# Layer-1 adaLN blocks on VectorE by multiply-and-sum along transposed weights, and layer-norm and square sums moved from GpSimd to VectorE

## The chip, the cores and the metric

One NeuronCore of a Trainium2 chip runs the whole kernel. The metric is the device time of one execution in microseconds; runs of the kernel before and of the changed one are compared by their medians.

## What is computed

Two transformer-like layers run over 384 tokens (128 context tokens, 256 sample tokens) of width 2048. Each layer has an adaLN modulation, one wide input projection that feeds two branches, and one output projection. All of it is fp32. The parts that the change touches:

```
def adaln(cond, w_mod, b_mod):
    m = jax.nn.silu(cond) @ w_mod + b_mod          # (1, 2048) @ (2048, 6144)
    shift, scale, gate = jnp.split(m, 3, axis=-1)
...
for layer in range(2):
    sh, sc, gt = adaln(cond_ctx, w_mod, b_mod)     # context tokens
    hp = rms_norm(xp, g) * (1.0 + sc) + sh
    sh2, sc2, gt2 = adaln(c, w_mod, b_mod)         # sample tokens
    ...
# layer 0, conv branch
a = ga * sigmoid(gb)
a = depthwise_conv(a, conv_w) + conv_b             # 31 taps, 1024 channels
a = silu(layer_norm(a, ln_g, ln_b)) * silu(gate_a)
# layer 0, attention branch: qk-RMSNorm, rotary, dense attention, times silu(gate_b)
# both: concat([a, b]) @ w_out, times gate, added to x
```

So each layer needs 12 vector blocks of adaLN (shift, scale and gate, four blocks of 512 outputs each), and each block is a product of two vectors of 2048 (context and sample condition) with a 2048 x 512 weight block of 4 MB.

## The kernel before, in words

Features lie on partitions (128 at a time, 16 blocks `k`), tokens on the free axis. Every projection (`proj_feat`, 256 output features) streams its weights from HBM in four pieces of 512 KB (`load_w`, pool `raw`, NRAW buffers, SP's queue). ScalarE rounds a piece to its high half `whi`, VectorE subtracts to get the low half `wlo` (both in `split`; three buffers each), and TensorE makes 24 matmuls of 128x384 per piece in `feat_unit` (L354: hi by hi, hi by lo, lo by hi). A piece is called a split below. Projections of layer 0 come in this order: four pairs gate `gb` and value `ga` of the conv branch, then four of gate A, four of gate B, then the eight of the output projection `out_proj`. Results lie in PSUM pairs `pf` (five banks).

Beside the projections, layer 0 has three chains. Attention (`qkv_tile`, `attend`) is emitted behind the second `ga`. The 31-tap convolution (`conv_steps`, L659 on VectorE) starts with each `ga`. When all eight channel blocks are convolved, layer norm follows: `ln_mean` sums the eight blocks into `lsum` and multiplies by ones on TensorE (`mean`), `ln_center` subtracts the mean (L711) and adds squares into `lvar`, `rstd_cols`/`rstd_rows` turn that into `rsl` (TensorE), a power on GpSimd, and `rbl` (TensorE), `ln_out` scales (L721), and L741 multiplies the branch into `mix`. Only then can `out_proj` split `mix` into `hhi`/`hlo` and begin. The buffers `wk` (four) are shared by the squares of the layer norm and by the SiLU results of gate B, in program order.

adaLN blocks are made in two ways. On TensorE: `gemv_block` loads 4 MB through the `raw` pool (SP's queue) and makes 16 matmuls (L139) and four transposes (L172); `pump` issues its pieces at a rate (`R0`, `RA`, `RB`) per unit of weights. On VectorE: `mod_vector` loads eight pieces of 512 KB through GpSimd's queue (`side_load`) into a ring of two slots and runs, for each of 16 `k` and both conditions, one instruction of 128x512 that multiplies by a per-partition scalar and adds to a running sum (L195 the first, L197 the rest). Its `done` transposes the sums on TensorE (`gvt`, L205, eight transposes) and reduces them on VectorE (L207). Layer 1's four shift blocks, the last scale block and four gate blocks are made that way, nine in all; their sums and slots lie in rooms that are free at the time (`mix`, `kT`, `v`, `att`, `apad`).

The order of the instructions on each engine is set by a list scheduler when the program is built: what is ready goes, by priority; the convolution taps and VectorE's adaLN work have a later priority (`later(LATER)`). On the chip each engine takes its own list strictly in order.

Of the kernel before, what the change touches and what calls it, by code (L numbers as in the profile page):

```python
# [19 lines left out]
P = 128  # L20
# [18 lines left out]
NRAW = 7  # L39
# [4 lines left out]
SHIFT_AT = (7, 9, 11)  # L44
RA = 1.35
# [6 lines left out]
def trunk(ctx: ExitStack, tc: tile.TileContext, d: dict, o: dict):  # L52
# [129 lines left out]
    def mod_vector(layer, part, j, av, ring):  # L182
        if (layer, part) not in mods:
            mod_tile(layer, part)
        w = d[f"mod_w{layer}"][4 * part + j]
        av = av.rearrange("p (g f) -> p g f", g=2)
        with later(LATER):
            for u in range(8):
                raw = ring[u % len(ring)].rearrange("p (k f) -> p k f", k=2)
                side_load(raw, w[:, 2 * u:2 * u + 2, :])  # L190
                for i in range(2):
                    k = 2 * u + i
                    for g in range(2):
                        if k == 0:
                            nc.vector.tensor_scalar(av[:, g], raw[:, i], cst[:, 2 * k + g:2 * k + g + 1], None, ALU.mult)  # L195
                        else:
                            nc.vector.scalar_tensor_tensor(av[:, g], raw[:, i], cst[:, 2 * k + g:2 * k + g + 1], av[:, g],  # L197
                                                           ALU.mult, ALU.add)

        def done():  # L200
            sl = slice(4 * j, 4 * j + 4)
            for g in range(2):
                pc = ps_gv.tile([P, 512], F32, tag="gv", name="gvt")
                for i in range(4):
                    ins = nc.tensor.transpose(pc[:, i * P:(i + 1) * P], av[:, g, i * P:(i + 1) * P], ident).ins  # L205
                    tc.add_manual_dep(ins, order["product"].name, NOSYNC, reason="not before its place")
                nc.vector.tensor_reduce(mods[layer, part][:, sl, g:g + 1], pc.rearrange("p (k c) -> p k c", k=4),  # L207
                                        AX.X, ALU.add)
            mod_finish(layer, part, sl, None)
        return done  # L210

# [31 lines left out]
    xT = big.tile([P, KC, T], F32, tag="bigA", name="xT")  # L243

    def square_sum():
        av = tmp.tile([P, T], F32, tag="sacc", name="sacc", bufs=1)

        def each(f):
            if f == 0:
                nc.scalar.activation(av, xT[:, f, :], AF.Square)  # L250
# [480 lines left out]
    for fb in range(4):  # L731
        def ev_a(j, ps, fb=fb):
            if fb == 0 and j == 0:
                shifts.pop(0)()
# [239 lines left out]
```

## Time and profile before

| | |
|---|---|
| three timed runs | 1295.45, 1299.06, 1300.13 us; median 1299.06 |
| profiled execution | span 1295.9 us from its first instruction to its last; the page gives no other time of it |
| busy | PE 98%, DVE 68%, ACT 42%, POOL 11% of the span |
| chain that ended last | PE 85%, DMA 5%, DVE 5%, issue 3% |
| DMA | 252.8 MB, 195 GB/s mean |

A row of a group reads: line, engine, operation, written tile `<-` read tiles, shape, count; then the time in which at least one of them ran (us), the mean of one (ns); then the engine's idle time just before them and what ended it. Busy time of TensorE counts overlapping matmuls as one, so 98% is no measure of its pace: two neighbouring 128x384 matmuls that each last 342 ns start 175 ns apart when nothing holds them.

### The profile page before, as it was taken

The page shows a single profiled execution, that of the slowest core. Times are in us where ns is not written, and L with a number is a line of the kernel's source. Part 1 is how long each engine was busy: PE and PEld are TensorE (multiplying, and loading weights), DVE is VectorE, ACT ScalarE, POOL GpSimd, SP SyncE. Part 2 cuts the span into 40 slices and gives each one's busy share as a digit, 9 for nine tenths or more (in the row PEclk, how much of TensorE's full clock was granted, in tenths as well). Part 3 has the DMA queues.
Part 4 walks back from the last instruction along what each step waited for, and adds up shares of the span by engine and source line. Part 5 has one row for each costly group of instructions (what it writes and reads, how often), then busy time and mean ns, then how long its engine had stood idle before and what let it go on. Part 6 is the DMA issues. An engine that isn't in the chain of part 4 may idle for free.

```text
span 1295.9 us, 18150 instructions
## 1 busy us (share of the span) xinstructions
PE 1267.4 (98%) x7000; PEld 1123.1 (87%) x7000; DVE 882.0 (68%) x1464; ACT 544.5 (42%) x941; POOL 142.2 (11%) x162
## 2 busy tenths in 40 slices
PE   6999999999999999999999999999999999999997
PEld 4566687888887888999999988899999999999997
DVE  2245627899999979989976932454544689996443
ACT  3344433644556645432363633344444422343332
POOL 0210100210000042122220000000000011111110
PEclk9999999999999999999999999999999999999998
DMA  9988867688654566676644444433333577764412
GB/s 364 403 309 313 300 185 258 232 307 295 226 166 160 196 221 218 209 225 217 199 135 130 121 128 130 123 118 109 98 99 103 185 231 229 252 194 146 123 50 98
DMA packets 71222, 252.76 MB, mean 195 GB/s; under 512 B 7456, under 2 KB 11808, under 8 KB 67552
## 3 DMA queue, kind: packets, MB, share of 16 engines
q1 hardware_dynamic: 59920, 211.90, 48.9%
q0 software_dynamic: 11072, 39.60, 9.8%
q8 instruction: 55, 0.90, 0.3%
q14 instruction: 31, 0.25, 0.1%
q10 hardware_dynamic: 144, 0.10, 0.0%
HBM read 247.91 MB, written 3.67 MB: 194 GB/s over the span
## 4 chain that ended last, share of the span: by engine, by line
PE 85%; DMA 5%; DVE 5%; issue 3%; POOL 1%; ACT 1%; SPq 0%; DVEq 0%; POOLq 0%; ACTq 0%
PE pf L354 57%; PE pt L333 10%; PE q L571 6%; PE gv L139 5%; DMA area<-in_mod_w 3%; DVE area L197 2%; PE s_ps L470 2%; PE o_ps L495 2%; DVE wlo L262 1%; DMA raw<-in_wf 1%; PE pT_ps L491 1%; DMA ring<-in_mod_w 1%; PE gv L172 1%; POOL lvar L718 1%; PE y_ps L862 1%
## 5 line engine op out<-in xcount | busy, mean ns | idle before, releaser
L354 PE MATMUL pf<-hhi,whi 128*128 128x384 f32 (+1 forms) x1664 | 569.2, 342 | 0.7 <-ACT whi L261 0.7
L354 PE MATMUL pf<-hlo,whi 128*128 128x384 f32 (+1 forms) x1664 | 569.7, 342 | 0.0
L354 PE MATMUL pf<-hhi,wlo 128*128 128x384 f32 (+1 forms) x1664 | 567.2, 343 | 1.7 <-DVE wlo L262 1.7
L262 DVE TENSOR_TENSOR wlo<-raw,whi 128x1024 fp32r<-128x1024 f32 x256 | 314.8, 1230 | 294.3 <-ACT whi L261 288.9
L261 ACT CAST whi<-raw 128x1024 fp32r<-128x1024 f32 x256 | 268.3, 1049 | 466.3 <-PE pf L354 242.5
L354 PEld LDWEIGHTS pf<-hhi,whi 128*128 128x128 f32 x1664 | 313.1, 188 | 24.0 <-issue 14.2
L354 PEld LDWEIGHTS pf<-hhi,wlo 128*128 128x128 f32 x1664 | 313.3, 188 | 9.8 <-issue 3.2
L354 PEld LDWEIGHTS pf<-hlo,whi 128*128 128x128 f32 x1664 | 313.6, 188 | 5.3 <-issue 2.9
L197 DVE SCALAR_TENSOR_TENSOR area<-area,cst 128x512 f32<-128x512 f32 x240 | 177.8, 777 | 14.7 <-DMA area<-in_mod_w 14.5
L659 DVE SCALAR_TENSOR_TENSOR cv<-apad,cw,cv 128x399 f32<-128x399 f32 x240 | 140.6, 635 | 1.1 <-ACT cv L657 0.8
L91 POOL DMA_DIRECT2D area<-in_mod_w x64 | 34.7, 542 | 424.0 <-DVE area L197 222.0
L333 PE MATMUL pt<-wlo,hhi 128*128 128x512 f32 x192 | 75.8, 395 | 0.0
L254 POOL TENSOR_TENSOR sacc<-sacc,sqf 128x384 f32<-128x384 f32 x43 | 55.2, 1284 | 186.9 <-ACT sqf L253 185.1
L333 PE MATMUL pt<-whi,hhi 128*128 128x512 f32 x192 | 75.7, 397 | 0.0
L333 PE MATMUL pt<-whi,hlo 128*128 128x512 f32 x192 | 75.0, 396 | 0.0
L333 PEld LDWEIGHTS pt<-whi,hhi 128*128 128x128 f32 x192 | 36.0, 188 | 12.4 <-ACT hhi L280 2.5
L571 PE MATMUL q<-whi,hhi 128*128 128x512 f32 x96 | 41.1, 428 | 4.4 <-ACT hhi L267 4.4
L478 ACT ACTIVATE pr<-s_ps,nm 128x384 f32<-128x384 f32 (+1 forms) x48 | 24.4, 509 | 49.7 <-DVE nm L477 34.7
L333 PEld LDWEIGHTS pt<-whi,hlo 128*128 128x128 f32 x192 | 36.0, 188 | 10.1 <-issue 0.8
L333 PEld LDWEIGHTS pt<-wlo,hhi 128*128 128x128 f32 x192 | 36.1, 188 | 9.0 <-issue 0.8
L139 PE MATMUL gv<-ring,cst 128*32 128x512 f32 (+1 forms) x288 | 35.8, 582 | 8.2 <-DMA ring<-in_mod_w 7.6
L571 PE MATMUL q<-wlo,hhi 128*128 128x512 f32 x96 | 40.5, 422 | 0.0
(171 smaller groups left out, 991.8 us busy)
## 6 DMA issues: line engine op xcount, KB each, us to landing
raw<-in_wf SPq DMA_DIRECT2D x144, 512.0 KB, 4.5
ring<-in_mod_w SPq DMA_DIRECT2D x32, 1024.0 KB, 7.5
area<-in_mod_w POOLq DMA_DIRECT2D x64, 512.0 KB, 4.6
raw<-in_w_out SPq DMA_DIRECT2D x64, 512.0 KB, 4.4
raw<-in_mod_w SPq DMA_DIRECT2D x56, 512.0 KB, 5.6
raw<-in_wq SPq DMA_DIRECT2D x32, 512.0 KB, 8.8
raw<-in_wt SPq DMA_DIRECT2D x24, 512.0 KB, 3.6
raw<-in_wkv SPq DMA_DIRECT2D x8, 512.0 KB, 7.8
```

The lines of the kernel that those rows point to most:

```text
L91: ins = nc.gpsimd.dma_start(dst, src).ins
L139: nc.tensor.matmul(ps[32 * g:32 * g + 32, :nf], lhsT=stat(k), rhs=raw[:, i % raw.shape[1], :], start=(k < 4), stop=(k >= KC - 4))
L197: nc.vector.scalar_tensor_tensor(av[:, g], raw[:, i], cst[:, 2 * k + g:2 * k + g + 1], av[:, g], ALU.mult, ALU.add)
L254: nc.gpsimd.tensor_tensor(av, av, s, ALU.add)
L261: nc.scalar.copy(dst_hi, src)
L262: order["split"] = nc.vector.tensor_tensor(dst_lo, src, dst_hi.bitcast(F32), ALU.subtract).ins
L333: nc.tensor.matmul(pp[t], lhsT=x[:, k, tt], rhs=y[:, i, :], start=(k == 0 and n == 0), stop=(k == KC - 1 and n == 2))
L354: ins = nc.tensor.matmul(pp[j][:, :n], lhsT=x[:, i, fj], rhs=y[:, k, :n], start=(begin and k % 8 == 0 and m == 0), stop=(end and k % 8 == ...
L470: nc.tensor.matmul(ps, lhsT=mix[:, h0 + h, t * P:(t + 1) * P], rhs=kT[:, kv, c0:c0 + nk * P], start=True, stop=True)
L495: nc.tensor.matmul(po, lhsT=v[:, slots[j], kv * HD:(kv + 1) * HD], rhs=pT[:, j, :], start=(j == 0), stop=(j == nk - 1))
L571: nc.tensor.matmul(pq[b][t], lhsT=x[:, k, tt], rhs=y[:, 0, 512 * b:512 * b + 512], start=(k == 0 and n == 0), stop=(k == KC - 1 and n == 2))
L659: nc.vector.scalar_tensor_tensor(st["o"], apad[:, c, j:j + CVW], cw[:, c, j:j + 1], st["o"], ALU.mult, ALU.add)
```

## The change

Eight things change together.

- `mod_vector` gives way to `mod_rows`: the modulation weights are also laid out transposed (`modT`, one output per partition), and the two silu'd conditions are kept in every partition (`crow`, 128 x 2 x 2048, two broadcast loads through GpSimd's queue and two SiLU on ScalarE). One `tensor_tensor_reduce` multiplies a 128 x n weight tile with a condition and sums along the free axis into one column of `sm`. n is 2048 (eight per block) or 1024 (sixteen per block, the halves added by L158).
- The four shift blocks use `lent`, the room of `x` (24 KB per partition: two load slots and one for the unread products), right after layer 0 has read `x` for the last time before its residual. `x` is loaded again (`xT2`, 3.1 MB) when they are done. They were the first block in `mix` and three in the rooms of layer norm's time.
- The scale's third block moves from TensorE to VectorE too, so two blocks (scale 2 and 3) use four rooms of 1024 (`kv`, which now holds `kT` and `v` as one, and two `att`). The gate's four blocks use `apad` and `kv`.
- No transposes `gvt` and no reductions L207 remain.
- `lsum`, `lvar` and layer 0's sum of squares `sacc` are added up by VectorE, not GpSimd.
- `NRAW` 7 becomes 6, `RA` 1.35 becomes 1.2, the places of the `done` calls change (`SCALE_AT`).
- Tile `x["T"]` stands for `xT`, since there are two.
- The scratch for GpSimd's DMA descriptors is set to 2048.

```
-NRAW = 7
+NRAW = 6
-SHIFT_AT = (7, 9, 11)
-RA = 1.35
+SCALE_AT = (11,)
+RA = 1.2
...
+    crow = const.tile([P, 2, D], F32, name="crow")
+    def load_crow():
+        for g, name in enumerate(("c_ctx", "c")):
+            side_load(crow[:, g, :], d[f"row_{name}"].rearrange("(a f) -> a f", a=1).broadcast_to([P, D]))
+        for g in range(2):
+            nc.scalar.activation(crow[:, g, :], crow[:, g, :], AF.Silu)
...
+    def mod_rows(layer, part, j, slots):
+        *slots, junk = slots
+        n = junk.shape[1]
+        sm = const.tile([P, 4, 2, D // n], F32, name=f"sm{layer}{part}{j}")
+        with later(LATER):
+            for i in range(4):
+                for h in range(D // n):
+                    raw = slots[turn["n"] % len(slots)]
+                    turn["n"] += 1
+                    side_load(raw, d[f"modT{layer}"][16 * part + 4 * j + i, :, h * n:(h + 1) * n])
                     for g in range(2):
-                        if k == 0:
-                            nc.vector.tensor_scalar(av[:, g], raw[:, i], cst[:, 2 * k + g:2 * k + g + 1], None, ALU.mult)
-                        else:
-                            nc.vector.scalar_tensor_tensor(av[:, g], raw[:, i], cst[:, 2 * k + g:2 * k + g + 1], av[:, g],
-                                                           ALU.mult, ALU.add)
+                        nc.vector.tensor_tensor_reduce(out=raw if g else junk, in0=raw, in1=crow[:, g, h * n:(h + 1) * n],
+                                                       scale=1.0, scalar=0.0, op0=ALU.mult, op1=ALU.add,
+                                                       accum_out=sm[:, i, g, h:h + 1])
...
-    gemv_q.extend(bias_q + mod_part(0, 2) + mod_part(1, 1, (512,) * 3))
+    gemv_q.extend(bias_q + mod_part(0, 2) + mod_part(1, 1, (512,) * 2))
+    lent = big.tile([P, KC * T], F32, tag="bigA", name="lent")
+    slots = [lent[:, i * D:(i + 1) * D] for i in range(3)]
+    shifts = [mod_rows(1, 0, j, slots) for j in range(4)]
...
+    room = big.tile([P, 2048], F32, tag="kv", name="area")
+    vring = [room[:, :1024], room[:, 1024:]] + [area("att", 3)[:, :1024] for _ in range(2)]
+    scales = [mod_rows(1, 1, j, vring) for j in (2, 3)]
     def ln_mean():
-            nc.gpsimd.tensor_tensor(av, av, apad[:, c, :T], ALU.add)
+            nc.vector.tensor_tensor(av, av, apad[:, c, :T], ALU.add)
...
-            nc.gpsimd.tensor_tensor(ln["v"], ln["v"], s, ALU.add)
+            nc.vector.tensor_tensor(ln["v"], ln["v"], s, ALU.add)
...
+    for done in shifts:
+        done()
+    x["T"] = big.tile([P, KC, T], F32, tag="bigA", name="xT2")
+    side_load(x["T"], d["xT"])
```

How the order of the instructions changes is seen at three places. Rows stand as the built programs list them, one engine each, in the order in which that engine takes them; a trailing x3 is a repeat, and the lines of the changed program count some lines more (L360 is L354, L268 is L262, L667 is L659, L720 is L711).

The first place is TensorE in gate B of layer 0, where the mean of the layer norm is made. Before:

```order
L495 MATMUL o_ps<-pT,v 128x512
L706 MATMUL mean<-lsum,ones 128x384
L354 MATMUL pf_4001<-hhi,whi 128x384
L354 MATMUL pf_4001<-hlo,whi 128x384
L354 MATMUL pf_4001<-hhi,wlo 128x384
```

and in the changed program:

```order
L360 MATMUL pf_4189<-hlo,whi 128x384
L360 MATMUL pf_4189<-hhi,wlo 128x384
L715 MATMUL mean<-lsum,ones 128x384
L226 MATMUL rsl<-ones,lvar 128x1 x3
L360 MATMUL pf_4190<-hhi,whi 128x384
L360 MATMUL pf_4190<-hlo,whi 128x384
```

Before, `rsl` stands 78 rows behind `mean`, with 75 projection matmuls between (the second half of gate B's first projection and most of its second). In the changed program `rsl` follows `mean` at once, in the middle of gate B's third projection (`pf_4189` and `pf_4190` are its pair).

The second place is VectorE at the same point, between the mean and the last addition to `lvar`. Before (L195 and L197 are adaLN work, `area` its rooms):

```order
L195 TENSOR_SCALAR area<-area,cst 128x512 x2
L197 SCALAR_TENSOR_TENSOR area<-area,cst 128x512 x6
L711 TENSOR_TENSOR apad<-apad,mean 128x384 x8
L197 SCALAR_TENSOR_TENSOR area<-area,cst 128x512 x2
L262 TENSOR_TENSOR wlo<-raw,whi 128x1024
L197 SCALAR_TENSOR_TENSOR area<-area,cst 128x512 x2
L262 TENSOR_TENSOR wlo<-raw,whi 128x1024
```

and in the changed program (the ISA rows are the multiply-and-sum and the read of its sum):

```order
L720 TENSOR_TENSOR apad<-apad,mean 128x384 x8
L207 ISA area,sm_3201<-area,crow 128x1024
L207 ISA sm_3201 128x1
L207 ISA area,sm_3201<-area,crow 128x1024
L207 ISA sm_3201 128x1
L727 TENSOR_TENSOR lvar<-lvar,sql 128x384
L207 ISA area,sm_3201<-area,crow 128x1024
L207 ISA sm_3201 128x1
L207 ISA area,sm_3201<-area,crow 128x1024
L207 ISA sm_3201 128x1
L727 TENSOR_TENSOR lvar<-lvar,sql 128x384
```

From the last addition to `lsum` to the last of seven to `lvar` the changed list holds 16 multiply-and-sums of 1024, eight subtractions of the mean and the seven additions, and no split of weights.

The third place is VectorE where the conv branch begins, behind the shifts of layer 0. Before:

```order
L392 TENSOR_TENSOR mix_1213<-rope,mix_1213 128x128
L397 TENSOR_TENSOR mix_1213<-rope,mix_1213 128x2x32 x2
L262 TENSOR_TENSOR wlo<-raw,whi 128x1024 x7
L637 TENSOR_TENSOR nat_772<-nat_772,gv 128x512
L262 TENSOR_TENSOR wlo<-raw,whi 128x1024
```

and in the changed program:

```order
L207 ISA lent,sm_1241<-lent,crow 128x2048
L207 ISA sm_1241 128x1
L268 TENSOR_TENSOR wlo<-raw,whi 128x1024 x2
L207 ISA lent,sm_1241<-lent,crow 128x2048
L207 ISA sm_1241 128x1
L207 ISA lent,sm_1241<-lent,crow 128x2048
L207 ISA sm_1241 128x1
L268 TENSOR_TENSOR wlo<-raw,whi 128x1024
```

Seven splits in a row with nothing between them are now mixed with multiply-and-sums of 2048. All 32 of the shift blocks stand between the first and the 28th split of layer 0's feature projections.

## Rows read from the trace of the kernel before

**Rows 1.** The page's busy times of the span.

```profile
span 1295.9 us, 18150 instructions
PE 1267.4 (98%) x7000; PEld 1123.1 (87%) x7000; DVE 882.0 (68%) x1464; ACT 544.5 (42%) x941; POOL 142.2 (11%) x162
```

**Rows 2.** Busy by stretch: length, PE, PEld, DVE, ACT, POOL, clock, DMA share, GB/s.

```profile
120.00:150.00 30.00, 29.65 (x157) 18.35 (x153) 17.06 (x41) 12.08 (x23) 0.00 (x0) 1.00 0.98 374
149.30:210.00 60.70, 60.06 (x338) 49.13 (x336) 24.54 (x46) 21.09 (x39) 5.86 (x7) 1.00 0.62 196
210.00:450.00 240.00, 238.67 (x1360) 195.41 (x1353) 224.90 (x383) 134.01 (x273) 19.22 (x21) 1.00 0.69 234
450.00:480.00 30.00, 30.00 (x171) 24.97 (x170) 21.86 (x30) 16.05 (x28) 12.87 (x11) 1.00 0.65 212
480.00:510.00 30.00, 27.87 (x162) 26.75 (x160) 29.46 (x50) 15.18 (x23) 7.34 (x9) 1.00 0.62 205
510.00:527.50 17.50, 16.24 (x92) 16.25 (x93) 17.50 (x29) 10.06 (x19) 4.03 (x3) 1.00 0.74 232
1020.00:1170.00 150.00, 150.00 (x859) 148.12 (x858) 141.03 (x204) 52.16 (x70) 18.17 (x31) 1.00 0.69 222
```

**Rows 3.** Chain that ended last, in order of time: start, us, what.

```profile
511.26 34.74 PE pf L354 x197
...
1133.13 43.51 PE pf L354 x248
```

**Rows 4.** Waits from 149.3 to 527.5: us in total, times, longest.

```profile
ACT whi L261 <- DMA raw<-in_wf: 71.4, 27, 8.6
DVE wlo L262 <- ACT whi L261: 52.9, 24, 10.7
```

**Rows 5.** Groups of VectorE by form, whole span.

```profile
L262 DVE TENSOR_TENSOR wlo<-raw,whi 128x1024 fp32r<-128x1024 f32 x256 | 314.8, 1230 | 294.3 <-ACT whi L261 288.9 <-PE pf L354 4.4 <-DMA raw<-in_wq 0.4
L197 DVE SCALAR_TENSOR_TENSOR area<-area,cst 128x512 f32<-128x512 f32 x240 | 177.8, 777 | 14.7 <-DMA area<-in_mod_w 14.5
L197 DVE SCALAR_TENSOR_TENSOR mix<-mix,cst 128x512 f32<-128x512 f32 x30 | 21.4, 738 | 0.0
L207 DVE TENSOR_REDUCE mod<-gvt 128x4 f32<-128x512 f32 x18 | 12.2, 680 | 4.6 <-PE gvt L205 4.6
L195 DVE TENSOR_SCALAR area<-area,cst 128x512 f32<-128x512 f32 x16 | 7.2, 482 | 3.4 <-DMA area<-in_mod_w 3.3
L721 DVE TENSOR_TENSOR apad<-apad,rb 128x384 f32<-128x384 f32 x8 | 3.8, 548 | 0.0
```

**Rows 6.** VectorE's timeline: a small instruction and the start of the next.

```profile
441.81 0.16 DVE L163 SCALAR_TENSOR_TENSOR mod<-mod,vecs 128x8 f32<-128x8 f32 x1
441.88 0.55 DVE L475 TENSOR_REDUCE nm<-s_ps 128x1 f32<-128x384 f32 x1
```

**Rows 7.** VectorE's timeline: the splits around the output projection's start.

```profile
149.28 1.23 DVE L262 TENSOR_TENSOR wlo<-raw,whi 128x1024 fp32r<-128x1024 f32 x1 [1.02 <-ACT whi L261]
...
523.52 1.22 DVE L262 TENSOR_TENSOR wlo<-raw,whi 128x1024 fp32r<-128x1024 f32 x1
```

**Rows 8.** TensorE's timeline: mean, rsl, and the output projection's first matmul (527.33).

```profile
466.90 0.81 PE L706 MATMUL mean<-lsum,ones 128*128 128x384 f32 x2
...
484.00 0.83 PE L220 MATMUL rsl<-ones,lvar 128*128 128x1 f32 x6 [0.78 <-POOL lvar L718]
...
527.33 0.34 PE L354 MATMUL pf<-hhi,whi 128*128 128x384 f32 x1
```

**Rows 9.** TensorE's timeline: three transposes gvt and the start of the next matmul.

```profile
404.67 0.49 PE L205 MATMUL gvt<-ident,mix 128*128 128x128 f32 x3
404.99 0.81 PE L470 MATMUL s_ps<-kT,mix 128*128 128x384 f32 x2
```

**Rows 10.** DMA issues on the page: count, KB each, median us to landing.

```profile
ring<-in_mod_w SPq DMA_DIRECT2D x32, 1024.0 KB, 7.5
area<-in_mod_w POOLq DMA_DIRECT2D x64, 512.0 KB, 4.6
```

More of the change, by code (lines that the diff above doesn't have):

```diff
@@ L180, in mod_part @@
         return units
-    def mod_vector(layer, part, j, av, ring):
+    crow = const.tile([P, 2, D], F32, name="crow")
[4 more added lines that the diff above has]
+            nc.scalar.activation(crow[:, g, :], crow[:, g, :], AF.Silu)
+    turn = {"n": 0}
+    def mod_rows(layer, part, j, slots):
         if (layer, part) not in mods:
@@ L200, in done @@
         def done():
             sl = slice(4 * j, 4 * j + 4)
[L202 to L208, printed above, removed]
@@ L209, in done @@
-            mod_finish(layer, part, sl, None)
+            if n == D:
+                nc.vector.tensor_copy(mods[layer, part][:, sl, :], sm[:, :, :, 0])
+            mod_finish(layer, part, sl, None if n == D else sm)
         return done
@@ L241, in rstd_rows, with square_sum @@
         return rb
-    xT = big.tile([P, KC, T], F32, tag="bigA", name="xT")
-    def square_sum():
+    x = {"T": big.tile([P, KC, T], F32, tag="bigA", name="xT")}
+    def square_sum(eng):
         av = tmp.tile([P, T], F32, tag="sacc", name="sacc", bufs=1)
@@ L410, in qkv_state @@
     def qkv_state(layer):
-        kT = big.tile([P, NKV, 512], F32, tag="kT", name="kT")
-        v = big.tile([P, 4, NKV * HD], F32, tag="v", name="v")
+        kv = big.tile([P, 2048], F32, tag="kv", name="kv")
+        kT = kv[:, :1024].rearrange("p (h c) -> p h c", h=NKV)
+        v = kv[:, 1024:].rearrange("p (s c) -> p s c", s=4)
         side_load(kT[:, :, P:2 * P], d[f"cache_k{layer}"])
@@ L600, in trunk @@
     load_tables()
+    load_crow()
     kT, v = qkv_state(0)
@@ L688, in trunk @@
             bg["rate"] = RA
-            room = mix[:, :8, :].rearrange("p c t -> p (c t)")
-            shifts = [mod_vector(1, 0, 0, room[:, 2048:], [room[:, :1024], room[:, 1024:2048]])]
     def area(tag, n):
@@ L695, in trunk @@
     ln = {}
-    vring = [area("att", 3)[:, :1024] for _ in range(2)]
-    sums = [area(tag, n) for tag, n in (("kT", 1), ("v", 1), ("att", 3))]
-    shifts += [mod_vector(1, 0, j, sums[j - 1][:, :1024], vring) for j in (1, 2, 3)]
+    room = big.tile([P, 2048], F32, tag="kv", name="area")
+    vring = [room[:, :1024], room[:, 1024:]] + [area("att", 3)[:, :1024] for _ in range(2)]
+    scales = [mod_rows(1, 1, j, vring) for j in (2, 3)]
     def ln_mean():
         av = tmp.tile([P, T], F32, tag="sacc", name="lsum", bufs=1)
-        nc.gpsimd.tensor_tensor(av, apad[:, 0, :T], apad[:, 1, :T], ALU.add)
+        nc.vector.tensor_tensor(av, apad[:, 0, :T], apad[:, 1, :T], ALU.add)
         for c in range(2, 8):
-            nc.gpsimd.tensor_tensor(av, av, apad[:, c, :T], ALU.add)
+            nc.vector.tensor_tensor(av, av, apad[:, c, :T], ALU.add)
         pm = aux("mean")
@@ L833, in trunk @@
         conv_pair(fb, False)
-    vring = [area(tag, n)[:, :1024] for tag, n in (("att", 3), ("apad", 1))]
-    sums = [area(tag, n) for tag, n in (("kT", 1), ("v", 1), ("att", 3), ("att", 3))]
-    gates = [mod_vector(1, 2, j, sums[j][:, :1024], vring) for j in range(4)]
+    vring = [t[:, i * 1024:(i + 1) * 1024] for t in (area("apad", 1), big.tile([P, 2048], F32, tag="kv", name="area"))
+             for i in range(t.shape[1] // 1024)]
+    gates = [mod_rows(1, 2, j, vring) for j in range(4)]
     def ev_db(c):
@@ L855, in trunk @@
     y = []
-    av, square = square_sum()
+    av, square = square_sum(nc.gpsimd)
     tail = []
@@ L924, in _layout @@
     out["vecs"] = np.concatenate([a[name].reshape(n, P).T for name, n in _VECS], axis=1)
+    for name in ("c_ctx", "c"):
+        out[f"row_{name}"] = a[name].reshape(-1)
+    for l in range(2):
+        out[f"modT{l}"] = a[f"mod_w{l}"].T.reshape(48, P, D)
     out["xT"] = _by_rows(np.concatenate([a["x_prompt"][0], a["x_sample"][0]]))
```

45 lines of the change are left out of this document (17 added, 28 removed).

## The prediction

> **What bounds the kernel now.** I read the page's busy shares first [rows 1]: TensorE 98%, VectorE 68%. Neither number says who waits for whom, so I went to the stretches [rows 2], then to the chain, then to the rows at the place where layer 0 ends. From 511 us on the chain is long runs of matmuls: 43.51 us for 248 of them is 0.175 us each, and 34.74 for 197 is 0.176 [rows 3]. That is the matmuls' own pace: behind the start of layer 0's output projection TensorE is the bound, and work on other engines is free as long as it is on time. Before that it is different. From 149.3 us (the last split before the conv branch's first weights) to the output projection's first matmul at 527.3 [rows 7, 8] the sixteen projections are 1536 matmuls, 270 us at pace, but the stretch lasts 378. VectorE is busy 24.5 of the 60.7 us to 210, then 224.9 of 240, 21.9 of 30, 29.5 of 30 and 17.5 of 17.5 [rows 2]. So VectorE has room before 210 and nearly none from there to 527; it splits every piece of weights, and it makes the taps, the layer norm and the branch's products without which the output projection can't start. What counts for the time is when VectorE gets through its list to that place; then TensorE's remaining work follows at pace.
>
> **What the change removes there.** Up to the output projection's first split the old list has 30 adaLN instructions in `mix` (21.4 us), 34 in `area` (177.8/240 = 0.741 us each, 25.2), six first ones (7.2/16 = 0.45, 2.7) and two reductions L207 (12.2/18 = 0.68, 1.4) [rows 5]: 50.7 us.
>
> **What it adds there.** Up to the same split the new list has 32 multiply-and-sums of 2048, 31 of 1024, 63 reads of their sums, and 14 additions of 384 that GpSimd did.
> - No row shows the new instruction. The nearest reads two fp32 tiles of 1024 from SBUF: L262 at 314.8/256 = 1.23 us; L721 with 384 costs 3.8/8 = 0.48 [rows 5]. The slope is 0.75/640 = 1.17 ns per element at most, 1.04 ns if the fixed part is 0.16 us. So 1.23 us for 1024 and 1.23 + 1.07 = 2.30 for 2048. 32 x 2.30 = 73.6 and 31 x 1.23 = 38.1.
> - The reads of 128x1: a small instruction lasts 0.16 us, but the next one starts 0.07 behind its start [rows 6]. Bounds 0 to 0.16, I take 0.07: 4.4 us.
> - 14 additions at 0.48: 6.7 us.
> Sum 122.8, less 50.7: **72 us more** for VectorE in front of the output projection. For a whole block the new way is cheaper (8 x 2.37 = 19 us or 16 x 1.30 = 21, against 30 x 0.741 + 2 x 0.45 = 23). The load grows because four shift blocks and nearly two scale blocks now lie in front of this place, where two blocks and a bit lay (30 and 34 instructions); the old list made the rest later, beside a TensorE at its pace, at no cost.
>
> **When VectorE gets there.** Busy time before, 149.3 to 527.5, is 318.3 us [rows 2]; the first output split ends at 524.7 [rows 7], so 315.5 to there. 315.5 + 72.1 = 387.6, and without one idle moment the split ends at 149.3 + 387.6 = 536.9 us, behind the old 524.7 although all 59.9 us of idle time are used up. It won't be without idle moments. VectorE's list is in order; it waited 52.9 us for ScalarE's halves, and ScalarE 71.4 us for weights [rows 4]. Where work was plentiful (210 to 450) it still idled 15.1 us on 224.9 busy, 6.7%. On the 320 us up to the mean that is 21 us; in the layer norm behind it there is always a multiply-and-sum in front, so nothing there. I take 20; ends 0 and 40 (the 16 loads of 1 MB through GpSimd's queue fall into a stretch at 196 to 234 GB/s [rows 2], 7.5 us was the landing of 1 MB [rows 10], and with two slots a late one holds the whole list).
>
> **Ahead of it.** The two broadcasts into `crow` are 2 MB in a stretch whose DMA share is 0.98 at 374 GB/s [rows 2]: 5.6 us if nothing gives, 0 if the rest of the stretch has slack. I take 3.
>
> 536.9 + 20 + 3 = 560 us. TensorE's first matmul came at 527.3, 2.6 us behind the end of the split's making; now it waits for the split. **The output projection starts 32.5 us later.** TensorE's pause shows at one place. `rsl` follows `mean` at once in its list. VectorE needs 16 x 1.30 + 8 x 0.48 + 7 x 0.48 = 28 us from the last addition to `lsum` to the last to `lvar`, so TensorE stands still some 27 us. Before, 17.1 us lay between [rows 8], full of matmuls, with 0.78 idle.
>
> **Behind it.** 64 transposes `gvt` are gone from the stretch at pace; three took 0.32 us [rows 9], so 0.107 each, 6.8 us won. The TensorE block that is gone (16 matmuls, four transposes) lies in the stretch that VectorE sets: 0. The gate blocks: 64 x 1.30 = 83 us in place of 4 x 23 = 92, beside a TensorE at pace from 1020 to 1170 [rows 2]: 0, up to 9 us cheaper cover. The second load of `x`, 3.1 MB, is three of the loads of 7.5 us [rows 10] and has some 200 us: 0. Six weight buffers in place of seven: at pace six pieces are 25 us of work against 4.6 us of landing [rows 10], 0; in front of 527 the 71.4 us of waits for weights could grow by a seventh, 10 us, which VectorE's list covers; I keep it for the upper end. The sums of squares on VectorE come when it is idle: 0.
>
> **Sum.** +32.5 - 6.8 = +25.7 us. The profiled span is 1295.9, the median 1299.06 (3.2 above it; the page shows nothing else around the span), and a difference holds for both: **1324.8, say 1325 us**. The ends: 0 waits, no delay by `crow` and free reads give 532.5 and +5.2 - 6.8 = -2 (1297); without the last of these 1302. 40 us of waits, 5.6 and dear reads (+5.5) give 588 and +60.7 - 6.8 = +54 (1353).
>
> **The rivals.**
> - *VectorE's new work all finds room* (idle near 0). For it: 36 us of idle time before 210, exactly where the first 16 multiply-and-sums stand. Against: half of these waits were for weights, and the loads add to them. Output projection at 537 to 540, 1302 to 1305 us: no change by the bound below. Chance 0.11.
> - *The multiply-and-sum is cheap* (the other side). If it ran at two elements per cycle, as a one-tile operation may (L195 takes 0.45 us for 512, less than L262's slope gives), 32 x 1.1 + 31 x 0.5 = 51 us fall off: 509, so 18 earlier, and 18 + 7 = 25 won: 1274 us. It decides from 1.8 us per 2048 on, where half of the 51 is gone and nothing is lost. Against it: every VectorE row with two SBUF tiles runs at one element per cycle [rows 5]. Chance 0.07.
> - *It runs at half rate.* The trace has no VectorE instruction that sums along its row beside two fp32 tiles. L197 reads two fp32 tiles from SBUF too and takes 0.741 us for 512 [rows 5], far less than two cycles each. If the sum halves the rate, 32 x 2.1 + 31 x 1.07 = 100 us more stand in front of the output projection, and the gate's 64 cost 68 more in a stretch with 9 + 9 to spare [rows 2], some 50: 1325 + 150 = 1475 us. Chance 0.08. [...]
>
> **How the numbers follow.** Two runs of this kernel can be told apart from about 0.5%, 6.5 us. The forecast has 0.74. The range 1302 to 1353 takes in the first rival and leaves out cheap (0.07), half rate (0.08) and some tails (0.05). Faster by over 0.5%: 0.07 + 0.02 for the forecast's lower tail, 0.09. Within 0.5%: 0.11 + 0.02, 0.13. Slower: 0.78.
>
> **What would show it.** Right: TensorE idle some 27 us between `mean` and `rsl`, with VectorE busy there; multiply-and-sums at 2.3 and 1.23 us; the output projection's first matmul near 560; from there the same pace as before, and some 7 us less of it. The clock may fall in that pause; it was 1.00 in all stretches shown. Wrong: a multiply-and-sum under 1.8 or over 3.5 us; the mean reached before 470; a TensorE that waits behind 600 us.

## The result, and the profile after

The changed kernel takes **1334.3 us** (median of four runs, 1332.7 to 1335.9) against 1299.6 of the kernel before in the same session (1295.5 to 1300.2): a ratio of **1.0278, 95% interval 1.0260 to 1.0297**. It is slower by 35 us. The forecast was 1325, with a range of 1302 to 1353.

The page of the changed kernel: busy times, shares of the span and instructions, to be read against [rows 1], and the granted clock in 40 slices of the span.

```profile
span 1333.0 us, 17785 instructions
PE 1269.1 (95%) x6892; PEld 1118.7 (84%) x6892; DVE 870.7 (65%) x1452; ACT 543.3 (41%) x940; POOL 100.4 (8%) x128
PEclk9999999999999997799999999999999999999999
```

TensorE does almost the same busy time in a span that is 37.1 us longer, and on the page one place stands out where its clock falls. The stretches around it, busy times as in [rows 2] (length, PE, PEld, DVE, ACT, POOL, clock, DMA share, GB/s), and TensorE's waits (total, times, longest) from 480 to 600 us:

```profile
149.30:573.20 423.90, 385.02 (x2073) 316.41 (x2066) 375.00 (x604) 193.01 (x378) 38.78 (x47) 0.96 0.67 234
510.00:540.00 30.00, 4.57 (x20) 3.99 (x19) 28.78 (x57) 7.21 (x13) 4.96 (x10) 0.60 0.51 161
```

```profile
PE rsl L226 <- DVE lvar L727: 25.4, 1, 25.4
PE pf L360 <- DVE wlo L268: 2.6, 1, 2.6
```

TensorE stands for 25.4 us between `mean` and `rsl`; in the 30 us around this pause VectorE is busy 28.8. Its timeline (start, us, instruction) says with what:

```profile
518.06 1.22 DVE L207 CUSTOM_DVE_ANT_0 area<-area,crow 128x1024 f32<-128x1024 f32 x1
519.21 0.08 DVE L207 DVE_READ_ACCUMULATOR2_ANT sm<- 128x1 f32 x1
519.21 0.55 DVE L727 TENSOR_TENSOR lvar<-lvar,sql 128x384 f32<-128x384 f32 x1
519.68 1.22 DVE L207 CUSTOM_DVE_ANT_0 area<-area,crow 128x1024 f32<-128x1024 f32 x1
520.82 0.08 DVE L207 DVE_READ_ACCUMULATOR2_ANT sm<- 128x1 f32 x1
```

Two multiply-and-sums of a scale block stand between each addition to `lvar` and the next. The read of the sum starts at the same moment as the next instruction (519.21): from the multiply-and-sum's start to the next instruction's is 1.15 us, less than the 1.22 that it lasts, so the read is free. VectorE's groups by form (count, then busy us and mean ns, then idle time before):

```profile
L207 DVE CUSTOM_DVE_ANT_0 area<-area,crow 128x1024 f32<-128x1024 f32 x96 | 113.7, 1219 | 6.9 <-PE o_ps L502 4.4 <-DMA area<-in_modT 2.4
L207 DVE CUSTOM_DVE_ANT_0 lent<-lent,crow 128x2048 f32<-128x2048 f32 x32 | 72.9, 2284 | 0.1
```

The prices are those of the forecast (2.30 and 1.23 us). Now the place that decides. Counting 96 matmuls to a projection in TensorE's timeline, the output projection's first is this one:

```profile
573.22 0.34 PE L360 MATMUL pf<-hlo,whi 128*128 128x384 f32 x1
```

So it begins at **573.2 us** where it began, by the same count, at 527.5 (one matmul behind the 527.33 of [rows 8]). That is 45.7 us later. Behind it the span has 1333.0 - 573.2 = 759.8 us left, against 1295.9 - 527.5 = 768.4 before: 8.6 us won. 45.7 - 8.6 = 37.1 is the whole difference of the spans. Every experiment below is read by these two numbers, the start of the output projection ("start") and what lies behind it ("rest").

### The profile page after: what moved, and what is told of

The parts are those of the page before. It is cut to its first block, busy times and chain, and to the rows that moved or that the text cites. A ratio compares the mean times of both kernels' runs of the same rounds, so it can differ in the third digit from the quotient of the medians.

```text
span 1333.0 us, 17785 instructions
## 1 busy us (share of the span) xinstructions
PE 1269.1 (95%) x6892; PEld 1118.7 (84%) x6892; DVE 870.7 (65%) x1452; ACT 543.3 (41%) x940; POOL 100.4 (8%) x128
## 3 DMA queue, kind: packets, MB, share of 16 engines
q1 hardware_dynamic: 58768, 207.71, 46.3%
q0 software_dynamic: 10352, 49.04, 10.6%
## 4 chain that ended last, share of the span: by engine, by line
PE 89%; issue 4%; DMA 4%; DVE 2%; POOL 0%; ACT 0%; POOLq 0%; SPq 0%; DVEq 0%; ACTq 0%
PE pf L360 61%; PE pt L339 10%; PE q L578 6%; PE gv L139 5%; DMA raw<-in_mod_w 2%; PE s_ps L477 2%; PE o_ps L502 2%; PE pT_ps L498 1%; DMA ring<-in_mod_w 1%; DMA raw<-in_wf 1%; PE gv L172 0%; POOL area L91 0%; DVE wlo L268 0%; PE qT_ps L463 0%; DVE area L207 0%
## 5 line engine op out<-in xcount | busy, mean ns | idle before, releaser
L360 PE MATMUL pf<-hhi,whi 128*128 128x384 f32 (+1 forms) x1664 | 571.4, 343 | 1.0 <-ACT whi L267 1.0
L360 PE MATMUL pf<-hlo,whi 128*128 128x384 f32 (+1 forms) x1664 | 570.7, 343 | 0.0
L360 PE MATMUL pf<-hhi,wlo 128*128 128x384 f32 (+1 forms) x1664 | 563.6, 343 | 3.7 <-DVE wlo L268 3.7
L268 DVE TENSOR_TENSOR wlo<-raw,whi 128x1024 fp32r<-128x1024 f32 x256 | 313.0, 1224 | 334.0 <-ACT whi L267 328.4
L360 PEld LDWEIGHTS pf<-hhi,wlo 128*128 128x128 f32 x1664 | 314.5, 189 | 19.9 <-DVE wlo L268 6.2
L360 PEld LDWEIGHTS pf<-hhi,whi 128*128 128x128 f32 x1664 | 314.5, 189 | 17.8 <-issue 9.6
L360 PEld LDWEIGHTS pf<-hlo,whi 128*128 128x128 f32 x1664 | 314.9, 189 | 4.9 <-issue 1.9
L667 DVE SCALAR_TENSOR_TENSOR cv<-apad,cw,cv 128x399 f32<-128x399 f32 x240 | 138.1, 626 | 0.0
L207 DVE CUSTOM_DVE_ANT_0 area<-area,crow 128x1024 f32<-128x1024 f32 x96 | 113.7, 1219 | 6.9 <-PE o_ps L502 4.4
L207 DVE CUSTOM_DVE_ANT_0 lent<-lent,crow 128x2048 f32<-128x2048 f32 x32 | 72.9, 2284 | 0.1
L91 POOL DMA_DIRECT2D area<-in_modT x48 | 25.5, 532 | 510.8 <-PE o_ps L502 189.6
L260 POOL TENSOR_TENSOR sacc<-sacc,sqf 128x384 f32<-128x384 f32 x28 | 33.5, 1196 | 175.2 <-ACT sqf L259 174.4
L139 PE MATMUL gv<-raw,cst 128*32 128x512 f32 x192 | 37.1, 613 | 7.2 <-DMA raw<-in_mod_w 5.3
L139 PE MATMUL gv<-ring,cst 128*32 128x512 f32 (+1 forms) x288 | 35.6, 582 | 8.5 <-DMA ring<-in_mod_w 7.6
```

Of the source, the lines that this page charges most:

```text
L91: ins = nc.gpsimd.dma_start(dst, src).ins
L139: nc.tensor.matmul(ps[32 * g:32 * g + 32, :nf], lhsT=stat(k), rhs=raw[:, i % raw.shape[1], :], start=(k < 4), stop=(k >= KC - 4))
L207: nc.vector.tensor_tensor_reduce(out=raw if g else junk, in0=raw, in1=crow[:, g, h * n:(h + 1) * n], scale=1.0, scalar=0.0, op0=ALU.mult, ...
L260: eng.tensor_tensor(av, av, s, ALU.add)
L268: order["split"] = nc.vector.tensor_tensor(dst_lo, src, dst_hi.bitcast(F32), ALU.subtract).ins
L360: ins = nc.tensor.matmul(pp[j][:, :n], lhsT=x[:, i, fj], rhs=y[:, k, :n], start=(begin and k % 8 == 0 and m == 0), stop=(end and k % 8 == ...
```

## The experiments

| kernel | median us | ratio to before, 95% | start | rest |
|---|---|---|---|---|
| before | 1299.6 | 1 | 527.5 | 768.4 |
| changed | 1334.3 | 1.0278 (1.0260 to 1.0297) | 573.2 | 759.8 |
| e1 scale sums short | 1318.9 | 1.0152 (1.0135 to 1.0169) | 557.9 | 759.8 |
| e2 shift sums short | 1303.2 | 1.0026 (1.0014 to 1.0037) | 542.4 | 759.5 |
| e3 both short | 1300.5 | 1.0010 (0.9999 to 1.0020) | 540.3 | 759.5 |
| e4 additions on GpSimd | 1330.0 | 1.0238 (1.0220 to 1.0257) | 568.2 | 759.8 |
| e5 before, six buffers | 1308.0 | 1.0081 (1.0066 to 1.0097) | 534.0 | 770.4 |
| e6 scale blocks late | 1314.4 | 1.0126 (1.0108 to 1.0144) | 553.6 | 760.0 |
| e7 two early, two late | 1308.1 | 1.0082 (1.0069 to 1.0095) | 547.8 | 759.9 |
| e8 blocks in the old places | 1310.3 | 1.0098 (1.0084 to 1.0113) | 548.4 | 760.3 |
| e9 changed, seven buffers | 1314.7 | 1.0123 (1.0109 to 1.0138) | 553.6 | 760.0 |
| e10 three early, three late, seven | **1286.6** | **0.9906 (0.9893 to 0.9920)** | 524.3 | 759.6 |
| e11 old places, seven | 1296.2 | 0.9977 (0.9968 to 0.9986) | 533.8 | 759.6 |
| e12 three early, three late, six | 1302.9 | 1.0031 (1.0020 to 1.0042) | 541.8 | 759.4 |

The kernel before was run again beside each group of experiments (medians of 1297.3 to 1299.3), and the ratios are to these; medians of different groups are compared to some 2 us.

The rest is 759.4 to 760.3 us in every kernel that has the new blocks, wherever they stand, and 768.4 to 770.4 in both that have the old ones. What differs among them is the start alone.

### Is it VectorE's time or the loads? (e1 to e4)

e1 and e2 shorten the sums of one kind of block and keep all loads; e3 does both.

```diff
...
+                        m = 8 if n < D and part == 1 else n        # e2: n == D, e3: part < 2
-                        nc.vector.tensor_tensor_reduce(out=raw if g else junk, in0=raw, in1=crow[:, g, h * n:(h + 1) * n],
+                        nc.vector.tensor_tensor_reduce(out=(raw if g else junk)[:, :m], in0=raw[:, :m], in1=crow[:, g, h * n:h * n + m],
```

> The multiply-and-sums of the two scale blocks read and multiply only 8 of their 1024 elements; their loads stay. Left out: most of the sums of scale blocks 2 and 3, so layer 1's scales are not what the reference asks. Theory A (VectorE's busy time in its list ahead of the output projection sets its start): 31 of these stand ahead of the output projection, at 1.15 us from start to next and some 0.15 us when short, so 31 us less; TensorE's pause between mean and rsl falls from 25.4 us to 10 or less, out0 starts near 542 in place of 573, and the run takes 1300 to 1307 us. Theory B (the loads, through contention and late weights, set it): nothing of that changes, 1328 to 1334 us.

> The multiply-and-sums of the four shift blocks read and multiply only 8 of their 2048 elements; their 16 loads of 1 MB stay. Left out: most of the sums of layer 1's shifts. Theory A: 32 x 2.28 us become 32 x 0.15, 68 us less for VectorE ahead of the output projection, most of which comes through because VectorE had 49 us of idle time in 424; some of it is lost to new waits for weights, as half of the place lies ahead of 210 us: out0 45 to 68 us earlier, 1266 to 1290 us. The pause of 25 us between mean and rsl stays, since its 16 multiply-and-sums belong to the scales. Theory B (the 16 MB and the broadcasts into crow delay the weights): at most 10 us come off, 1322 to 1334 us.

> Both of the above: the sums of shift and scale blocks are short, all loads stay. Left out: most of layer 1's shifts and of its scale blocks 2 and 3. Theory A: some 100 us less for VectorE ahead of the output projection; then it is not VectorE alone that sets the place, so less than the sum of the two runs above comes off: 70 to 95 us, 1240 to 1265 us, and the pause between mean and rsl is under 10 us. Theory B: 1318 to 1334 us.

Measured: 15.3, 31.0 and 33.8 us less. In e1 the wait of `rsl` falls to 10.6 us, and in e3 it is gone. So VectorE's time is the larger part of the loss, and theory B falls as the main cause. But theory A fell too, in its size: e1, e2 and e3 were to come out at 1300 to 1307, 1266 to 1290 and 1240 to 1265, and all three missed. Taking both away gives 33.8 and not 15.3 + 31.0 = 46.3. With some 88 us less of VectorE's busy time than the changed kernel, e3 doesn't even reach the start of the kernel before (540.3 against 527.5). From 149.3 us to the start in e3:

```profile
149.30:540.30 391.00, 378.34 (x2076) 315.18 (x2075) 286.98 (x620) 183.62 (x372) 37.48 (x51) 0.98 0.72 256
```

VectorE is busy 287.0 of 391 us, so the length of its list doesn't set the start any more; TensorE is busy 378.3 (overlapping matmuls count as one and their ends are modelled, so this is an upper bound of its work). Something other than VectorE's time costs 12.8 us at the start. Much of it is lost between 210 and 300 us, first the kernel before, then e3:

```profile
210.00:300.00 90.00, 88.67 (x533) 73.18 (x526) 84.08 (x143) 46.42 (x129) 13.02 (x13) 1.00 0.81 275
```

```profile
210.00:300.00 90.00, 80.41 (x418) 61.81 (x419) 84.10 (x185) 48.82 (x145) 13.01 (x14) 0.92 0.86 317
```

There TensorE starts 418 matmuls where it started 533, and its granted clock is 0.92. Why wasn't separated: the smaller ring, the early loads and `crow` are all still in e3.

e4 puts the additions of the layer norm and of the squares of `x` back on GpSimd (`nc.vector` to `nc.gpsimd` in `ln_mean`, `ln_center` and `square_sum`).

> The additions of the layer norm and of the squares of x go back to GpSimd, nothing else is changed. Theory A: 14 x 0.48 = 6.7 us less for VectorE ahead of the output projection, but its chain of additions then runs on GpSimd and the multiply-and-sums between them still stand on VectorE, so 0 to 7 us come off: 1327 to 1335 us. Theory C (moving the additions is what costs, since they now stand behind multiply-and-sums in VectorE's list): the pause of 25 us goes and 20 us or more come off, 1314 us or less.

Measured: 4.3 us less, as A has it. The pause stays (17.9 us, now for GpSimd's `lvar`). Theory C falls: where the additions run is a minor matter.

### The ring of weight buffers (e5, e9)

The change also takes a weight buffer away, to make room for `crow`. e5 does that alone in the kernel before:

```diff
-NRAW = 7
+NRAW = 6
```

> The kernel before with six weight buffers in place of seven, nothing else. If the smaller ring is part of what the two short runs could not give back (out0 at 540 to 542 us there against 527.5 before, with 70 to 100 us of VectorE's sums gone), it costs 5 to 13 us: 1304 to 1312 us. If six buffers are enough, as the forecast took it, 1298 to 1302 us.

Measured: **10.7 us slower**. The forecast had put 0 here. (In the profiled executions the start is 6.5 us later and the rest 2.0 longer.) e9 gives the changed kernel its seventh buffer back; the room comes from the rope table and small tiles:

```diff
-NRAW = 6
+NRAW = 7
...
-    rope = const.tile([P, 2, 2, HD], F32, name="rope")
...
+        rope = room[:, 256:768].rearrange("p (i t c) -> p i t c", i=2, t=2)      # layer 0, in spare room of mix
+        side_load(rope, d["rope"])
...
+    tables["rope"] = tmp.tile([P, 512], F32, tag="gs", name="rope", bufs=1).rearrange("p (i t c) -> p i t c", i=2, t=2)   # layer 1
+    side_load(tables["rope"], d["rope"])
...
-        m = const.tile([P, KC, 2], F32, name=f"mod{layer}{part}")
+        m = mods[0, part] if layer else const.tile([P, KC, 2], F32, name=f"mod{part}")
```

The gate blocks share small tiles for their sums as well; in e9 (not in e10 and e11) block 2 of layer 1's gate thereby takes block 3's sums, with the same instructions in the same number.

> The changed kernel with seven weight buffers again; the room for the seventh comes from the rope table (loaded into spare room for each layer) and from sharing small tiles between the layers. Nothing is left out. If the ring's cost adds to VectorE's, as the 10.7 us of the run of the kernel before with six buffers would have it: 1320 to 1327 us. If VectorE's list hides it, because TensorE waits for VectorE and not for weights while the list is too long: 1330 to 1336 us.

Measured: **19.6 us faster** than the changed kernel, 1314.7; the better end of the first guess was 14 us. How a missing buffer reaches TensorE can be read in the changed kernel. The chain of waits there, pieces in order of time (start, us, what):

```profile
236.51 1.08 PE gv L139 x8
237.60 5.46 DMA raw<-in_mod_w
243.06 0.04 issue
243.10 1.92 PE gv L139 x4
```

The load at 237.60 starts when TensorE is through with a buffer's contents, and lands 5.46 us later; TensorE makes the few matmuls that stand ahead of that block in its list, then stands for 3.0 us until 243.10. The buffers are used in a ring, by the splits and by TensorE's adaLN blocks alike. What the queue of these loads waits for, from 150 to 560 us in the changed kernel (total, times, longest), is that a split or a matmul of such a block frees one:

```profile
SPq L98 <- DVE wlo L268: 203.3, 46, 40.6
SPq L98 <- PE gv L139: 104.2, 34, 9.9
```

The same 15 us in the two kernels, first with six buffers, then with seven:

```profile
235.00:250.00 15.00, 9.79 (x50) 6.13 (x52) 15.00 (x19) 9.85 (x32) 7.75 (x6) 0.89 0.82 307
```

```profile
235.00:250.00 15.00, 13.66 (x82) 9.99 (x82) 15.00 (x21) 9.99 (x30) 5.05 (x5) 1.00 0.89 324
```

With six, TensorE starts 50 matmuls and its granted clock is 0.89 (1.00 up to 242 us, 0.72 from 242 to 244, 0.50 from 244 to 246 and 0.93 from 246 to 248, behind the standstill); with seven it starts 82 at 1.00. ScalarE's waits for weights from 150 to 480 us fall as well, first with six, then with seven:

```profile
ACT whi L267 <- DMA raw<-in_wf: 62.4, 14, 10.2
```

```profile
ACT whi L272 <- DMA raw<-in_wf: 21.5, 11, 7.6
```

Their sum is no measure of the price by itself: the kernel before has 71.4 us of them [rows 4], and 54.3 with six buffers (e5), where it is slower. In e9 most of what is left is VectorE's list: `rsl` still waits 20.3 us for `lvar`, and the start comes at 553.6, 26.1 us behind the kernel before.

### Where the blocks stand (e6, e7, e8)

e6 holds the loads of the two scale blocks until the last product of `mix` and `apad`, so that the blocks stand beside the output projection:

```diff
-    scales = [mod_rows(1, 1, j, vring) for j in (2, 3)]
...
-        nc.vector.tensor_tensor(mix[:, c, :], mix[:, c, :], apad[:, c, :T], ALU.mult)
+        product = nc.vector.tensor_tensor(mix[:, c, :], mix[:, c, :], apad[:, c, :T], ALU.mult).ins
+    held, order["hold"] = order["hold"], product
+    scales = [mod_rows(1, 1, j, vring) for j in (2, 3)]
+    order["hold"] = held
```

> The changed kernel with full sums, the two scale blocks' loads held until the last product of mix and apad, so that their 32 multiply-and-sums stand beside the output projection, where VectorE was busy 72 us of 135. Nothing is left out. If their place is what costs, this gives what the short scale sums gave: out0 near 558 us, the run 1316 to 1322 us. If a block of multiply-and-sums costs its time wherever it stands, 1330 to 1336 us.

Measured: 19.8 us less than the changed kernel with every sum still made. The start comes at 553.6 and the rest stays at 760.0: beside a TensorE at its pace the blocks are free, ahead of the output projection they are not. It gains even more than was expected and than e1 (15.3), where the loads and short sums stayed; which of these makes the difference wasn't tried.

e7 keeps two shift blocks early, holds two in the same way, and gives the scale blocks to TensorE (four blocks there). e8 has x, blocks and TensorE's three adaLN blocks where the kernel before has them, with `mod_rows` in place of `mod_vector`.

```diff
-    gemv_q.extend(bias_q + mod_part(0, 2) + mod_part(1, 1, (512,) * 2))
+    gemv_q.extend(bias_q + mod_part(0, 2) + mod_part(1, 1))                # e7; e8: (512,) * 3
-    shifts = [mod_rows(1, 0, j, slots) for j in range(4)]
+    shifts = [mod_rows(1, 0, j, slots) for j in range(2)]                  # e7
...
+    late = [mod_rows(1, 0, j, vring) for j in (2, 3)]                      # e7, held as in e6
...
+            shifts = [mod_rows(1, 0, 0, [room[:, i * 1024:(i + 1) * 1024] for i in range(3)])]    # e8, in mix
...
+    shifts += [mod_rows(1, 0, j, vring) for j in (1, 2, 3)]                # e8, then scale block 3
```

> The changed kernel with two shift blocks in x's room, two held until the last product, both scale blocks back on TensorE (four blocks there, one more than before) and the additions on GpSimd. VectorE has 315.5 - 50.7 + 16 x 2.32 = 302 us ahead of the output projection, 13.5 less than before; TensorE has one block more there, 16 matmuls and four transposes, some 3 us; behind it the 64 transposes gvt are gone, 6.8 us. If VectorE's list alone set the place before: 1280 to 1288 us. If TensorE and the weights were nearly as tight there, as the two short runs suggest: 1290 to 1300 us.

> The kernel before's placing (x stays, one shift block in mix, three behind, scale block 3 last, three blocks on TensorE, additions on GpSimd) with the multiply-and-sum blocks in place of the old ones, six weight buffers and crow. VectorE's load ahead of the output projection falls by some 4 us, the 64 transposes behind it are gone, 6.8 us: 1287 to 1294 us if the blocks themselves cost nothing more than the old ones; 1298 or more if the broadcasts into crow, the smaller ring or the loads cost what the transposes give.

1308.1 and 1310.3, where at most 1300 and 1294 were hoped for: e7 missed both of its ranges, and of e8's two cases the second came true. The rest is the expected 760 in both; the start is 20 us behind that of the kernel before, although VectorE has hardly more to do ahead of it (322.5 and 318.4 us, against 318.3). Both have six buffers. How much of it is the ring, e11 tells for e8; for e7 it wasn't tried.

### Both causes undone (e10, e11, e12)

e10: seven buffers as in e9; three shift blocks early in the lent room; both scale blocks and the last shift block held as in e6; additions on GpSimd. e12 is the same with six buffers and the rope table in its old place. e11 is e8 with seven buffers as in e9.

```diff
-    shifts = [mod_rows(1, 0, j, slots) for j in range(4)]
+    shifts = [mod_rows(1, 0, j, slots) for j in range(3)]
...
+    late = [mod_rows(1, 1, 2, vring), mod_rows(1, 1, 3, vring), mod_rows(1, 0, 3, vring)]
```

> Seven buffers, three shift blocks in x's room, both scale blocks and the last shift block held until the last product of mix and apad, two blocks on TensorE, additions on GpSimd. VectorE has 315.5 - 50.7 + 24 x 2.32 = 320.5 us ahead of the output projection, 5 more than before; TensorE has one block less there; behind it the transposes are gone, and 48 multiply-and-sums, 55 us, must fit into some 63 us that VectorE has idle beside the output projection. If the causes are VectorE's place in the list and the ring: 1284 to 1297 us. If the held blocks come too late for layer 1, or the early loads cost what they save: 1300 us or more.

> The blocks in the places they had before (the eighth run's kernel) with seven buffers. If the ring's cost is the same here as in the kernel before: 1310.3 - 10.7 = 1299.6, so 1296 to 1302 us. If the loss of that run is in the blocks' waits for their loads around the layer norm instead: 1305 to 1311 us.

> The tenth run's placing with six weight buffers: it completes the table of two placings by two rings (changed kernel 1334.3 with six, 1314.7 with seven; this placing 1286.6 with seven). Theory A (a buffer comes free when VectorE has split its piece, so the price of the missing buffer grows with how long the pieces stand behind other work in VectorE's list: 10.7 us in the kernel before, 19.6 in the changed kernel): some 10 us here, where VectorE's load is near that of the kernel before, 1294 to 1300 us. Theory B (the price is that of the ring alone and the same in every placing): 19 us or more, 1304 to 1309 us. Theory C (TensorE is the bound here, so that the buffer is worth little): under 1291 us.

Measured: e10 **1286.6 us, 0.9906 of the kernel before**, faster than both. e10's page, its stretch from 149.3 us to the start, and the stretch beside the output projection in which the three held blocks run:

```profile
span 1283.9 us, 17844 instructions
PE 1255.3 (98%) x6892; PEld 1114.9 (87%) x6892; DVE 870.4 (68%) x1439; ACT 543.4 (42%) x938; POOL 143.3 (11%) x162
```

```profile
149.30:524.30 375.00, 369.83 (x2075) 311.10 (x2074) 328.52 (x516) 192.43 (x375) 46.67 (x47) 1.00 0.68 239
570.00:700.00 130.00, 130.00 (x745) 129.99 (x744) 100.03 (x174) 51.84 (x85) 27.30 (x25) 1.00 0.55 174
```

VectorE does the work of the changed kernel (870.4 us busy against 870.7) in a span that is 49 us shorter. TensorE's clock is 1.00 in both stretches, and the held blocks leave its pace alone (745 matmuls in 130 us, 0.174 us each). e10 keeps `crow`, the transposed weights, 12 of the 16 early loads of 1 MB, the second load of `x`, `RA` and the scratch of the changed kernel, so with seven buffers none of these makes a kernel slow.

e11 came out at 1296.2, 14.1 us under e8: the ring once more. Its start is still 6.3 us behind that of the kernel before, with no more VectorE time ahead of it (316.4 us); TensorE waits 2.8 us for `rbl` and 1.8 for a split there, and the rest wasn't traced. e12 fell between its theories: 16.3 us for the missing buffer, where A had some 10 and B 19 or more. In four placings the buffer (with the edits that make room for it, outside the kernel before) is worth 10.7, 14.1, 16.3 and 19.6 us; all but the first compare two groups, so neighbouring values are hardly apart. The two higher values belong to the kernels with 1 MB loads early in the stretch. In e12 the standstill at 240 us is there too (the row of those 15 us, and that of the stretch up to the start):

```profile
235.00:250.00 15.00, 10.02 (x50) 6.18 (x52) 15.00 (x20) 9.90 (x31) 7.53 (x6) 0.89 0.83 305
149.30:541.80 392.50, 379.45 (x2070) 313.84 (x2067) 336.33 (x532) 187.57 (x373) 50.58 (x49) 0.99 0.66 231
```

The first row is nearly that of the changed kernel. It doesn't tell loads and sums apart: the first three shift blocks are early in both, and VectorE is busy 72.7 us from 149.3 to 235 in the changed kernel and 72.8 in e12; the 38.7 us by which its busy time up to the start differs (375.0 - 336.3) lie behind. e2 and e3 tell more. They have six buffers and all early loads, but short early sums. From 150 to 300 us TensorE's adaLN blocks (L139) wait 0.8 and 1.4 us for a load there, against 3.8 in the changed kernel, 3.7 in e1 and 7.2 in e12, and the standstill of 3 us near 240 is gone: from 150 to 480 us no wait of TensorE in e3 is longer than 1.7 us. It isn't undisturbed there: in shorter pieces it stands for 3.5 of the 10 us from 240, and its clock is 0.80 from 245 to 250 and 0.52 from 250 to 255. So the loads alone don't make this one long wait; the long sums belong to it. What the buffer is worth without them stays open: no kernel was run with short sums and seven buffers, nor with the early sums and without their loads.

## Why the prediction was right, and which of its steps failed

The direction, the place and the range were right; the sum was 10 us short. That it came so near is in part luck, since two errors offset each other: up to the start VectorE's load was put 12.6 us too high (387.6 against 375.0) and its idle time 25.9 too low (23 against 48.9). By its steps:

- **The price of the multiply-and-sum: right.** 2.284 and 1.219 us against 2.30 and 1.23, which is 1.04 ns for each element more, the lower of the forecast's two slopes, so both the cheap and the half-rate rival are refuted. The half rate was an assumption that no row of the kernel before shows, and for this summing form with two fp32 tiles no halving shows in the rows of the changed kernel. (No row gives a cycle either. The rates that the prediction counts in cycles are, in the trace of the kernel before, 1.04 ns for each element more in a two-tile addition, L408 with 1214 ns for 1024 and 412 for 256, and 0.51 ns in a one-tile product, L889 with 746 for 1024 and 487 for 512.) The reads were to cost 4.4 us and cost nothing, and neighbouring instructions overlap by 0.07.
- **VectorE's load ahead of the start: a little too large.** 72 us more were forecast. The rows give 375.0 us from 149.3 to the start against 318.3 before, 56.7 more. Free reads and the overlap, 32 x 0.16 + 31 x 0.15 = 9.8, are most of the gap of 15.4. Of the other 5.6, 2.6 are the old instructions in `area` (34 took 27.8 us there, not 25.2) and 2.5 the taps, which the forecast took as unchanged (140.6 us before, 138.1 after):

```profile
L197 DVE SCALAR_TENSOR_TENSOR area<-area,cst 128x512 f32<-128x512 f32 x34 | 27.8, 854 | 0.0
```

- **The ring: this step failed.** "Six weight buffers in place of seven: at pace six pieces are 25 us of work against 4.6 us of landing [rows 10], 0; in front of 527 the 71.4 us of waits for weights could grow by a seventh, 10 us, which VectorE's list covers; I keep it for the upper end." It costs 10.7 us in the kernel before and 19.6 in the changed one, so VectorE's list covers none of it. That a later piece makes a later split, and a later split frees its buffer later, fits the queue's waits above; it wasn't tried apart. The sum had 20 us of waits and 3 for `crow`; VectorE is idle 423.9 - 375.0 = 48.9 us ahead of the start, and 37.6 in e9. Load and waits together gave 560 and came to 573.2. With seven buffers the start is 553.6, so the forecast of the start was 6 us too late for the kernel that it had reckoned with and 13 too early for the one that it got.
- **VectorE sets the start: right in the changed kernel by way of the pause, wrong for the one before.** The prediction set 270 us for the projections' matmuls against a stretch of 378 and took the rest for room that VectorE's list fills. The projections share the stretch with attention and TensorE's adaLN blocks: TensorE's busy times in [rows 2] from 149.3 to 527.5 add up to 372.8 of 378.2 us, and the chain in [rows 3] has it in one run of matmuls from 511.26 to 546, across the start. So the old start did not wait for the first output split. In the changed kernel it doesn't either: from 480 to 600 us TensorE waits for VectorE twice, 25.4 us at `rsl` and 2.6 at a split of gate B at 555.4, then runs on through 573.2. The step "now it waits for the split" is thus not what happened; VectorE's list holds TensorE some 36 us earlier, at `rsl`, and gate B's remaining matmuls follow, the first of them at a lower clock (0.87 from 540 to 565). Taking the early sums away gave 33 us at the start, with six buffers (e3), although VectorE's busy time fell by 88.
- **TensorE's pause: right.** 25.4 us against 27, at the place named, behind the additions named. The clock fell there too, to 0.60 over the 30 us from 510. e6 takes most of the pause away (9.0 us left) and the start is 19.6 us earlier.
- **Behind the start: right, a little too small.** 6.8 us were forecast for the 64 transposes, and 8.6 measured; the rest of 759.4 to 760.3 in twelve kernels says that it belongs to the new blocks and not to where they stand. That it is the transposes wasn't tried apart. The second load of `x` and the squares cost nothing, as forecast: the rest is the same without them (e8, e4). The gate blocks are in all twelve, so their part can't be read from it.
- **The additions on VectorE:** 6.7 us of load were reckoned; putting them back gave 4.3 (e4).

How the 45.7 us at the start divide: the seventh buffer alone gives back 19.6, the short sums alone 32.9; together that is 52.5, more than there is. So each is dearer beside the other, and a single split of the loss into two terms would be invented. What the trace does show is where TensorE stood: of the 45.7 us, 24.6 are the longer wait at `rsl` (25.4 against 0.78).

## What to carry to other kernels

Before work is moved to an engine that looks idle, add up the other engine's busy time over the same stretch: here TensorE stood idle for only 5 of the 378 us ahead of the output projection, so it was hardly waiting for anything there that a shorter list could bring. (A matmul of 342 ns that starts 175 ns behind its neighbour at pace can stand further from it without showing as idle, so TensorE's real room is larger by an amount that wasn't measured; the best start of all, e10's, is 3.2 us earlier.) Work that nobody needs yet belongs behind the last thing that others wait for; one dependency on its loads (e6) moved it there and was worth 20 us. A buffer given up to pay for a table is a cost of the change like any other, and must be tried by itself on the old kernel.

## What the runs showed of the hardware

- The multiply-and-sum along a row of two fp32 tiles takes 1.04 ns for each element more (1219 ns for 1024, 2284 for 2048), and the read of its sum (81 ns) lies wholly beside the next instruction.
- One buffer of 512 KB in a ring of seven was worth 10.7 to 19.6 us, though TensorE at its pace needs a piece only every 4.2 us (24 matmuls, 0.175 us apart) and such a piece lands in 4.0 to 4.5 (medians of `raw<-in_wf`: 4.5 before, 4.0 in the changed kernel, 4.2 in e5). In the stretch that is mixed with adaLN blocks, the loads wait for VectorE and TensorE to free a buffer (203.3 and 104.2 us from 150 to 560 in the changed kernel), and TensorE then stood for part of one landing (3.0 of 5.46 us from 237.60).
- Such a standstill of 3 us at 240 was followed by a stretch at a lower granted clock (0.89 over 15 us, in the changed kernel and e12). With seven buffers (e9, e10) there was neither: from 235 to 250 us the clock was 1.00, and TensorE stood for 1.3 us in e9 and 0.5 in e10.
